# Summing the first pair's biases on ScalarE and queueing its query projection behind the spreading of 1/rms in a two-layer decoder trunk

## The chip, the cores and the metric

The kernel runs on one core of one Trainium2 chip. The metric is the device time of one launch in microseconds (us); three runs of the kernel before were timed, and one further execution was profiled. Engines are named as the profile names them: PE (TensorE matmul), PEld (its weight loads), DVE (VectorE), ACT (ScalarE), POOL (GpSimd) and SP (SyncE, which issues the DMAs here). "L178" is line 178 of the kernel before.

## The reference, cut to what matters

The input is a residual stream x of 1024 tokens by 1024 channels and a conditioning vector c. Layer A is a gated short convolution: modulated RMS norm, a projection to four parts, a causal convolution over three tokens, gates, an output projection, and the residual. Layer B is stick-breaking attention with 16 heads of 64 channels. Its keys and values come from a modulated norm of the same stream that layer B normalises.

```python
def modulated_norm(x, g, shift, scale):
    return rmsnorm(x, g) * (1.0 + scale[:, None, :]) + shift[:, None, :]
...
hkv = modulated_norm(x, kv_norm_g, kv_shift, kv_scale)
k_flat, v_flat = jnp.split(hkv @ w_kv, 2, axis=-1)
...
h = modulated_norm(x, norm_g, shift, scale)
q, z = jnp.split(h @ w_qz, 2, axis=-1)
...
return rmsnorm(x + gate[:, None, :] * (o @ w_out), final_norm_g)
```

## The kernel before, in words

Channels lie on the 128 partitions, tokens along the free dimension, in two halves of 512 tokens (`halves()`). Every matrix operand is split into a high and a low part in float32r, and a product is the sum of three matmuls (`linear`, L181 to L187): high weights by high activations (L185), high weights by low activations (L186), low weights by high activations (L187). One projection of 128 output channels over one half has 8 channel tiles, so 24 matmuls of 128x512, into one PSUM tile. PSUM tiles have four tags, "mm", "z", "tr" and "o", with two buffers each; `ps_any` goes round "mm", "z", "tr".

The change touches the seam between layer A's output projection and layer B's first pair of heads:

- The output projection of layer A (L432 to L457) runs per half over 8 output tiles. Each PSUM tile is added to the residual by DVE (L442), squared by ACT (L448), and the squares are summed by DVE (L450), all but those of the last tile.
- Then, in a high-priority block, `rms_columns` (L190) takes the column totals on PE: 8 matmuls of one column, four over the sum of the squares and four over the last tile's squares (L105; recorded as two groups). Twelve small DVE instructions follow (L202 to L209: a scaling, a shift, a subtraction, three Newton steps of three). `row_block` (L212) spreads the four columns of 1/rms over all partitions with four PE transposes (L215) and keeps the last of them as `last["pe"]`. DVE multiplies the eight residual tiles by it (L455), ACT rounds them to the high part x1h (L456), and DVE forms the low part x1l (L457).
- The weights of layer B's first pair (pair 0: keys, queries, values) are loaded while the second half of the output projection runs (`first_raw`, L460). `shift_terms` multiplies each by the modulation's shift and sums over the 8 channel tiles into a 128x128 tile (`bacc`), DVE multiplies the weights by the gain (L163), and `parts` (L469) splits them, ACT the high part and POOL the low part. The value weights' parts live in the attention pool, whose memory is that of layer A's tiles.
- A projection's bias is what is left of the shift: `shift_bias` (L174) transposes `bacc` on PE into a PSUM tile (L177), and DVE sums it along the free dimension (L178). `with_bias` (L494) hands it over as a function that is called at the first use. For pair 0 the PSUM tile has the tag "mm".
- `project_qkv(0)` (L567 to L573) walks the two halves: keys, queries, values. `evacuate` (L519) adds the bias, ACT for the high part (L521), DVE for the low part (L522); values go through ACT (L554), POOL (L556), four transposes (L559) and a second split. DMAs on SP's queue move the halves of the heads to their places (L517). In the first half the x1h and x1l that they read have long been made; in the second half they wait for L455 to L457.
- `attention` (L588) then takes the scores of a block of queries (L609, L610), the sigmoid on ACT (L614), a running product along the keys on DVE (L618), transposes (L628) and the product with the values (L642, L643).

The order of the instructions on each engine is laid out ahead of time by a planner: it takes the ready instruction of the highest priority (a high-priority block first, otherwise program order) by times that it models itself, and inserts the semaphores. Each engine then runs its list in order. `tc.issue_after(ins)` holds those instructions of its block that are on the engine of `ins` behind `ins` in that engine's list. `issue_after(last["x1"])` at L155 already keeps the next weights' DVE work behind L457.

Of the kernel before, what the change touches and what calls it, by code (L numbers as in the profile page):

```python
# [11 lines left out]
AF = mybir.ActivationFunctionType  # L12
ALU = mybir.AluOpType
AX = mybir.AxisListType.X

P = 128
# [21 lines left out]
def decoder_kernel(ctx, tc, vecs, xT, a_mod, kv_mod, b_mod, w_in, w_out_a, w_kv, w_qz, w_out_b, outT):  # L38
    nc = tc.nc
# [10 lines left out]
    last = {}  # L50

    def ps_tile(tag):
        return psum.tile([P, HALF], F32, name=f"ps_{tag}", tag=tag, bufs=PS_BUFS[tag])

    def ps_any():
        tags = ("mm", "z", "tr")
        seq[0] += 1
        return ps_tile(tags[seq[0] % len(tags)])
# [22 lines left out]
    def raw_tile():  # L81
        return wpool.tile([P, KT * P], F32, name="raw", tag="raw", bufs=3)
# [88 lines left out]
                acc, raw[:, kt * P:(kt + 1) * P], shift[:, kt:kt + 1], acc, op0=ALU.mult, op1=ALU.add)  # L171
        return acc

    def shift_bias(acc, tag):  # L174
        bias = const.tile([P, 1], F32, name="bias", tag="bias", bufs=8)
        ps = ps_tile(tag)
        nc.tensor.transpose(ps[:, :P], acc, ident)  # L177
        nc.vector.tensor_reduce(bias, ps[:, :P], AX, ALU.add)  # L178
        return bias

    def linear(ps, w, ah, al, sl, kts=range(KT)):  # L181
        hi, lo = w
        for kt in kts:
            wh, wl = hi[:, kt * P:(kt + 1) * P], lo[:, kt * P:(kt + 1) * P]
            nc.tensor.matmul(ps, lhsT=wh, rhs=ah[kt][:, sl], start=(kt == kts[0]), stop=False)  # L185
            nc.tensor.matmul(ps, lhsT=wh, rhs=al[kt][:, sl], start=False, stop=False)  # L186
            nc.tensor.matmul(ps, lhsT=wl, rhs=ah[kt][:, sl], start=False, stop=(kt == kts[-1]))  # L187


    def rms_columns(ssq, lo_t=0, hi_t=T, more=None, total=None):  # L190
# [36 lines left out]
    def halves():  # L227
        return [slice(h * HALF, (h + 1) * HALF) for h in range(NH)]
# [6 lines left out]
    def stile():  # L235
        return tmp.tile([P, HALF], F32, name="s", tag="s", bufs=11)
# [37 lines left out]
    for kt in range(KT):  # L274
# [16 lines left out]
        with tc.high_priority():  # L291
            for i in range(KT):
                nc.tensor.matmul(ssq[:, i:i + 1], lhsT=xr[:, i * P:(i + 1) * P], rhs=one,
                                 start=(kt == 0 and i == 0), stop=(kt == KT - 1 and i == KT - 1))
# [91 lines left out]
    for j in range(KT):  # L386
# [37 lines left out]
        if 2 <= j < 2 + len(PARTS):  # L424
            name, w, part, bcol, gcol = PARTS[j - 2]
# [6 lines left out]
    for sl in halves():  # L432
        ssq1 = tmp.tile([P, HALF], F32, name="ssq1", tag="graw", bufs=3)
        xs = []
        for j in range(KT):
            w = load_weights(w_out_a[j])[1:]
            xr = stile()
            xs.append(xr)
            nc.sync.dma_start(xr, xT[j * P:(j + 1) * P, sl])
            ps = ps_any()  # L440
            linear(ps, w, yh, yl, sl)
            nc.vector.scalar_tensor_tensor(xr, ps, mods["gate_a"][:, j:j + 1], xr, op0=ALU.mult, op1=ALU.add)  # L442
            nc.sync.dma_start(x1_dram[j, :, sl], xr)
            if j == 0:
                nc.scalar.activation(ssq1, xr, AF.Square)
            else:
                sq = tmp.tile([P, HALF], F32, name="sq1", tag="graw", bufs=3)
                nc.scalar.activation(sq, xr, AF.Square)  # L448
                if j < KT - 1:
                    nc.vector.tensor_add(ssq1, ssq1, sq)  # L450
        with tc.high_priority():

            scale = row_block(rms_columns(ssq1, 0, HALF, sq), 0, 4)
            for kt, x in enumerate(xs):
                nc.vector.tensor_mul(x, x, scale)  # L455
                nc.scalar.activation(x1h[kt][:, sl], x, AF.Copy)  # L456
                last["x1"] = nc.vector.tensor_tensor(x1l[kt][:, sl], x, x1h[kt][:, sl].bitcast(F32), op=ALU.subtract)  # L457
        if sl.start == 0:

            def first_raw(raw, w, m):  # L460
                nc.sync.dma_start(raw, w)
                return raw, scaled(raw, mods["gain_" + m], mods["shift_" + m])

            firsts = [
                first_raw(tmp.tile([P, D], F32, name="raw1", tag="gacc", bufs=1), w_kv[0], "kv"),
                first_raw(tmp.tile([P, 2 + T], F32, name="raw1", tag="v", bufs=2)[:, :T], w_qz[0], "b"),
                first_raw(raw_tile(), w_kv[NPAIR], "kv")]

    def parts(raw, pool=wpool, tags=("whi", "wlo"), bufs=2):  # L469
        hi, lo = (pool.tile([P, KT * P], F32R, name=n, tag=t, bufs=bufs) for n, t in zip(("whi", "wlo"), tags))  # L470
        split(hi, lo, raw, nc.gpsimd)
        return hi, lo

    first_w = [parts(raw) for raw, _ in firsts[:2]]
    papw.close()

# [17 lines left out]
    def with_bias(w, terms):  # L494
        bias = []

        def late():

            if not bias:
                bias.append(shift_bias(terms, "mm"))  # L500
            return bias[0]
        return w, late

    def projected(w, sl, ps_get=lambda: ps_tile("mm")):
        ps = ps_get()
        linear(ps, w, x1h, x1l, sl)
        return ps

    def half(a):
        return slice(a * DH, (a + 1) * DH)  # L510

    def project_qkv(p):
        def qk_tile(name):
            return att.tile([P, T], F32R, name=name, tag="qk", bufs=10)

        def move(dst, src):
            nc.sync.dma_start(dst.bitcast(F32), src.bitcast(F32))  # L517

        def evacuate(src, bias, hi, lo):  # L519
            bias = bias()  # L520
            nc.scalar.activation(hi, src, AF.Identity, bias=bias)  # L521
            nc.vector.scalar_tensor_tensor(lo, src, bias, hi.bitcast(F32), op0=ALU.add, op1=ALU.subtract)  # L522

        A, B = half(0), half(1)

        kl = [qk_tile("kl") for _ in range(2)]
        kh = [qk_tile("kh") for _ in range(2)]

        def keys(sl, t, bias):
            evacuate(t, bias, kh[0][:, sl], kl[0][:, sl])  # L530
            for k in (kh, kl):
                move(k[1][A, sl], k[0][B, sl])
                move(k[1][B, sl], k[0][B, sl])
                move(k[0][B, sl], k[0][A, sl])


        qq = [qk_tile("qq") for _ in range(2)]

        def queries(sl, t, bias):
            ql = att.tile([P, HALF], F32, name="ql", tag="pt", bufs=2).bitcast(F32R)  # L540
            evacuate(t, bias, qq[0][:, sl], ql)
            move(qq[1][B, sl], qq[0][B, sl])
            move(qq[1][A, sl], ql[B])
            move(qq[0][B, sl], ql[A])

        vv = []

        def values(sl, src, bias):

            if sl.start == 0:  # L550
                nc.gpsimd.memset(vt[:, :1], 0.0)
            else:
                nc.gpsimd.tensor_copy(vt[:, :1], vt[:, HALF:])
            nc.scalar.activation(vt[:, 1:], src, AF.Identity, bias=bias())  # L554
            t = att.tile([P, HALF], F32, name="dv", tag="pt", bufs=2)
            nc.gpsimd.tensor_tensor(t, vt[:, :HALF], vt[:, 1:], op=ALU.subtract)  # L556
            ps = ps_tile("tr")
            for i in range(4):
                nc.tensor.transpose(ps[:, i * P:(i + 1) * P], t[:, i * P:(i + 1) * P], ident)  # L559

            v = att.tile([P, 4, 4, DH], F32R, name="vv", tag="vv", bufs=4)
            src = ps.rearrange("p (b a d) -> p b a d", b=4, a=2)
            nc.scalar.activation(v[:, :, 0::3, :], src, AF.Copy)
            nc.vector.tensor_tensor(v[:, :, 1:3, :], src, v[:, :, 0::3, :].bitcast(F32), op=ALU.subtract)
            vv.append(v)

        if p == 0:  # L567
            first_w.append(parts(firsts[2][0], att, ("vv", "vv"), 4))
            (kw, kb), (qw, qb), (vw, vb) = (with_bias(w, terms) for w, (_, terms) in zip(first_w, firsts))
            for sl in halves():  # L570
                keys(sl, projected(kw, sl, ps_any), kb)
                queries(sl, projected(qw, sl, ps_any), qb)
                values(sl, projected(vw, sl, ps_any), vb)  # L573
        else:
            kw, kb = prepared(w_kv[p], mods["gain_kv"], mods["shift_kv"])
            for sl in halves():
                keys(sl, projected(kw, sl), kb)
            qw, qb = prepared(w_qz[p], mods["gain_b"], mods["shift_b"])
            for sl in halves():
                queries(sl, projected(qw, sl), qb)  # L580
            vw, vb = prepared(w_kv[NPAIR + p], mods["gain_kv"], mods["shift_kv"])
            for sl in halves():
                values(sl, projected(vw, sl), vb)
        return [(kh[a], kl[a], qq[a]) for a in range(2)], vv
# [152 lines left out]
    for j in range(EARLY):  # L737
        for sl in halves():
            ps = ps_any()
# [27 lines left out]
    for c, (a, b) in enumerate(CHUNKS):  # L767
        sl = slice(a, b)
# [51 lines left out]
```

## Time and profile before

| | us |
|---|---|
| three timed runs | 1450.73, 1195.78, 1192.18 |
| median of the three | 1195.78 |
| the profiled execution, its own time | 1193.45 |
| its span, first to last instruction | 1191.6 |

The time of the profiled execution and its span differ by 1.85 us, which lie outside the instructions. In that span PE is busy for 1160.2 us (97%), DVE for 857.4 (72%), ACT for 457.6 (38%) and POOL for 351.7 (30%); 36% of the time of the 16 DMA engines is used. The chain of work that ended last is PE for 86% and DVE for 10% of the span. Shares are averages over stages with different limits, so the seam has to be read from the timelines of the engines in its own stretch. A timeline row has start, length, engine, line, operation, output and inputs, shapes, count, and in brackets the idle time before it with what ended it. Matmuls overlap in it: each row's length holds the passage through the array, so the time that one takes on PE is the distance to the next start.

### The profile page before, as it was taken

What the parts mean: (1) busy time and instruction counts of PE and PEld (TensorE: products, weight loads), DVE (VectorE), ACT (ScalarE), POOL (GpSimd) and SP (SyncE); (2) the same over time, 40 slices, a digit from 0 to 9 for tenths busy, and PEclk for the clock granted to TensorE, in tenths of its full rate; (3) what the DMA queues carried; (4) which work ended last, traced back from release to release, by engine and by line L of the source; (5) the groups of instructions that cost most, each with busy time, mean ns of one, the idle gap of its engine ahead of it and who ended that gap; (6) DMA issues with size and microseconds to landing.
All of it is one profiled execution on the core that took longest, in us unless ns stands there. A gap on an engine that the chain in (4) does not pass through costs nothing.

```text
span 1191.6 us, 15883 instructions
## 1 busy us (share of the span) xinstructions
PE 1160.2 (97%) x6004; PEld 987.6 (83%) x6004; DVE 857.4 (72%) x1271; ACT 457.6 (38%) x750; POOL 351.7 (30%) x205
## 2 busy tenths in 40 slices
PE   7999999999999999989999999999999999999995
PEld 6888888888888888868888888888888888887885
DVE  7679325446546487478898898888988888686466
ACT  4344211212212224234544545444545444454341
POOL 3014423433433453321231322303123032121424
PEclk9799999999999999989999999999999999999997
DMA  9534315345354544342313223132241323562204
GB/s 373 220 123 144 104 54 165 109 151 176 99 167 150 193 141 154 114 100 70 86 65 89 63 78 99 64 85 67 63 107 53 84 67 79 143 248 88 71 1 141
DMA packets 61436, 138.47 MB, mean 116 GB/s; under 512 B 7472, under 2 KB 11696, under 8 KB 61360
## 3 DMA queue, kind: packets, MB, share of 16 engines
q1 hardware_dynamic: 61360, 137.46, 36.5%
q8 instruction: 47, 0.77, 0.3%
q14 instruction: 29, 0.24, 0.1%
HBM read 103.87 MB, written 14.68 MB: 99 GB/s over the span
## 4 chain that ended last, share of the span: by engine, by line
PE 86%; DVE 10%; issue 2%; ACT 1%; DMA 0%; DVEq 0%; SPq 0%; ACTq 0%
PE ps_mm L185 12%; PE ps_mm L186 12%; PE ps_mm L187 12%; PE ps_z L186 5%; PE ps_z L187 5%; PE ps_z L185 5%; PE ps_tr L186 5%; PE ps_tr L187 5%; PE ps_tr L185 5%; PE ps_tr L628 4%; DVE sfx L618 3%; PE ps_o L643 3%; PE ps_o L642 2%; PE ps_z L610 2%; PE ps_z L609 2%
## 5 line engine op out<-in xcount | busy, mean ns | idle before, releaser
L144 POOL TENSOR_TENSOR wlo<-raw,whi 128x1024 fp32r<-128x1024 f32 x87 | 219.4, 2523 | 632.9 <-ACT whi L143 516.2
L618 DVE TENSOR_TENSOR_SCAN sfx<-sfx,floor 128x128 f32<-128x128 f32 (+2 forms) x192 | 226.0, 1197 | 18.2 <-ACT sfx L614 18.2
L185 PE MATMUL ps_mm<-x1h,whi 128*128 128x512 f32 x480 | 191.7, 399 | 4.1 <-DVE bias L178 4.1
L186 PE MATMUL ps_mm<-x1l,whi 128*128 128x512 f32 x480 | 190.1, 396 | 0.0
L187 PE MATMUL ps_mm<-x1h,wlo 128*128 128x512 f32 x480 | 188.8, 393 | 0.0
L143 ACT ACTIVATE whi<-raw 128x1024 fp32r<-128x1024 f32 x87 | 92.1, 1059 | 144.1 <-issue 39.6
L631 ACT ACTIVATE ah<-ps_tr,minus 128x512 fp32r<-128x512 f32 (+1 forms) x160 | 100.4, 646 | 109.5 <-PE ps_tr L628 107.9
L632 DVE SCALAR_TENSOR_TENSOR al<-ps_tr,ah 128x512 fp32r<-128x512 f32 (+1 forms) x160 | 97.6, 623 | 41.7 <-ACT ah L631 41.2
L614 ACT ACTIVATE sfx<-ps_z 128x128 f32<-128x128 f32 (+2 forms) x192 | 90.4, 492 | 77.9 <-PE ps_z L610 76.2
L185 PEld LDWEIGHTS ps_mm<-x1h,whi 128*128 128x128 f32 x480 | 90.6, 189 | 22.2 <-DVE bias L178 5.1
L187 PEld LDWEIGHTS ps_mm<-x1h,wlo 128*128 128x128 f32 x480 | 90.6, 189 | 17.7
L121 DVE SCALAR_TENSOR_TENSOR gacc<-graw,cs,gacc 128x512 f32<-128x512 f32 x84 | 72.5, 885 | 44.9 <-DMA graw<-b_mod 22.1
L186 PEld LDWEIGHTS ps_mm<-x1l,whi 128*128 128x128 f32 x480 | 90.6, 189 | 16.6 <-DVE x1l L457 0.3
L628 PE MATMUL ps_tr<-ident,sfx 128*128 128x128 f32 x576 | 88.1, 274 | 0.0
L643 PE MATMUL ps_o<-al,vv 128*128 128x256 f32 x320 | 82.7, 294 | 4.3 <-DVE al L632 4.3
L642 PE MATMUL ps_o<-ah,vv 128*128 128x256 f32 x320 | 86.4, 282 | 0.1
L643 PEld LDWEIGHTS ps_o<-al,vv 128*128 128x128 f32 x320 | 60.4, 189 | 11.7 <-DVE al L632 8.7
L609 PE MATMUL ps_z<-kh,qq 128*128 128x128 f32 (+1 forms) x192 | 68.9, 364 | 0.7 <-ACT sfx L614 0.7
L642 PEld LDWEIGHTS ps_o<-ah,vv 128*128 128x128 f32 x320 | 60.5, 189 | 7.3 <-ACT ah L631 0.6
L628 PEld LDWEIGHTS ps_tr<-ident,sfx 128*128 128x128 f32 x576 | 65.5, 141 | 1.0
L610 PE MATMUL ps_z<-kl,qq 128*128 128x128 f32 (+1 forms) x192 | 65.3, 349 | 0.0
L185 PE MATMUL ps_mm<-nh,whi 128*128 128x512 f32 x152 | 59.4, 391 | 0.0
(277 smaller groups left out, 2435.0 us busy)
## 6 DMA issues: line engine op xcount, KB each, us to landing
raw<-w_in SPq DMA_DIRECT2D x29, 512.0 KB, 4.2
graw<-b_mod SPq DMA_DIRECT2D x48, 256.0 KB, 3.1
stage<-a_mod SPq DMA_DIRECT2D x16, 512.0 KB, 9.8
s<-xT SPq DMA_DIRECT2D x32, 256.0 KB, 4.8
graw<-kv_mod SPq DMA_DIRECT2D x32, 256.0 KB, 3.4
raw<-w_qz SPq DMA_DIRECT2D x16, 512.0 KB, 3.9
raw<-w_out_a SPq DMA_DIRECT2D x16, 512.0 KB, 3.5
raw<-w_kv SPq DMA_DIRECT2D x16, 512.0 KB, 3.6
```

Of the source, the lines that this page charges most:

```text
L143: nc.scalar.activation(hi, full, AF.Copy)
L144: lo_eng.tensor_tensor(lo, full, hi.bitcast(F32), op=ALU.subtract)
L185: nc.tensor.matmul(ps, lhsT=wh, rhs=ah[kt][:, sl], start=(kt == kts[0]), stop=False)
L186: nc.tensor.matmul(ps, lhsT=wh, rhs=al[kt][:, sl], start=False, stop=False)
L187: nc.tensor.matmul(ps, lhsT=wl, rhs=ah[kt][:, sl], start=False, stop=(kt == kts[-1]))
L609: nc.tensor.matmul(zps[:, :w], lhsT=qq[:, qs], rhs=kh[:, c0:c0 + w], start=True, stop=False)
L618: nc.vector.tensor_tensor_scan(rev, rev, floor[:, z0:z0 + w][:, ::-1], sf[r][:, s0 + w:s0 + w + 1], op0=ALU.mult, op1=ALU.max)
L628: nc.tensor.transpose(tp[:, s * P:(s + 1) * P], rows[r][:, jb * P - c0:(jb + 1) * P - c0], ident)
L631: nc.scalar.activation(ah[:, :w], tp[:, :w], AF.Identity, bias=minus)
L632: nc.vector.scalar_tensor_tensor(al[:, :w], tp[:, :w], -1.0, ah[:, :w].bitcast(F32), op0=ALU.add, op1=ALU.subtract)
L642: nc.tensor.matmul(ops[:, cols], lhsT=vs, rhs=ah[:, rs], start=first, stop=False)
L643: nc.tensor.matmul(ops[:, cols], lhsT=vs, rhs=al[:, rs], start=False, stop=end)
```

## The change

The bias of pair 0 is summed by an ACT copy with an accumulated output, in place of a DVE reduction; its PSUM tile has the tag "tr" in place of "mm". All three are traced right behind the second half's high-priority block, in a high-priority block of their own, with the transposes held behind the last matmul of the output projection. The two query projections of pair 0 (24 matmuls each) are held behind `last["pe"]`, the last transpose of the second half's spreading of 1/rms.

```diff
-    def shift_bias(acc, tag):
+    def shift_bias(acc, tag, eng=nc.vector):
         bias = const.tile([P, 1], F32, name="bias", tag="bias", bufs=8)
         ps = ps_tile(tag)
         nc.tensor.transpose(ps[:, :P], acc, ident)
-        nc.vector.tensor_reduce(bias, ps[:, :P], AX, ALU.add)
+        if eng is nc.scalar:
+            nc.scalar.activation(acc, ps[:, :P], AF.Copy, accum_out=bias)
+        else:
+            nc.vector.tensor_reduce(bias, ps[:, :P], AX, ALU.add)
         return bias
...
-            nc.tensor.matmul(ps, lhsT=wl, rhs=ah[kt][:, sl], start=False, stop=(kt == kts[-1]))
+            last["mm"] = nc.tensor.matmul(ps, lhsT=wl, rhs=ah[kt][:, sl], start=False, stop=(kt == kts[-1]))
...
+        out_last = last["mm"]
         with tc.high_priority():
...
+    with tc.high_priority(), tc.issue_after(out_last.ins):
+        first_b = [shift_bias(terms, "tr", nc.scalar) for _, terms in firsts]
     first_w = [parts(raw) for raw, _ in firsts[:2]]
...
-            (kw, kb), (qw, qb), (vw, vb) = (with_bias(w, terms) for w, (_, terms) in zip(first_w, firsts))
+            (kw, kb), (qw, qb), (vw, vb) = ((w, lambda b=b: b) for w, b in zip(first_w, first_b))
             for sl in halves():
                 keys(sl, projected(kw, sl, ps_any), kb)
-                queries(sl, projected(qw, sl, ps_any), qb)
+
+                with tc.issue_after(last["pe"].ins):
+                    q = projected(qw, sl, ps_any)
+                queries(sl, q, qb)
                 values(sl, projected(vw, sl, ps_any), vb)
```

## Rows read from the trace of the kernel before

**Rows 1.** Busy time of each engine over the whole span, from the page.

```profile
PE 1160.2 (97%) x6004; PEld 987.6 (83%) x6004; DVE 857.4 (72%) x1271; ACT 457.6 (38%) x750; POOL 351.7 (30%) x205
```

**Rows 2.** Stretches: PE, PEld, DVE, ACT, POOL busy; PE clock; DMA share; GB/s.

```profile
480.00:560.00 80.00, 75.62 (x350) 62.20 (x349) 51.41 (x99) 25.56 (x41) 21.23 (x13) 0.96 0.31 87
560.00:700.00 140.00, 138.91 (x789) 120.37 (x789) 126.39 (x191) 70.93 (x129) 38.11 (x24) 1.00 0.28 76
```

**Rows 3.** Timeline of PE across the seam.

```profile
494.14 0.39 PE L185 MATMUL ps_mm<-x1h,whi 128*128 128x512 f32 x1
...
494.60 0.27 PE L177 MATMUL ps_mm<-ident,bacc 128*128 128x128 f32 x1
494.71 0.95 PE L105 MATMUL ps_o<-one,ssq 128*128 128x1 f32 x8
...
500.18 0.94 PE L105 MATMUL ps_o<-one,sq 128*128 128x1 f32 x8
...
501.55 0.40 PE L185 MATMUL ps_z<-x1h,whi 128*128 128x512 f32 x1
...
507.14 0.60 PE L215 MATMUL ps_o<-ident,ry 128*128 128x128 f32 x4
507.69 0.33 PE L177 MATMUL ps_mm<-ident,bacc 128*128 128x128 f32 x1
509.18 0.50 PE L185 MATMUL ps_z<-x1h,whi 128*128 128x512 f32 x1 [1.17 <-ACT x1h L456]
512.90 0.80 PE L185 MATMUL ps_mm<-x1h,whi 128*128 128x512 f32 x1 [3.22 <-DVE bias L178]
...
517.93 0.63 PE L187 MATMUL ps_z<-x1h,wlo 128*128 128x512 f32 x1
```

**Rows 4.** Timeline of DVE across the seam.

```profile
501.17 0.16 DVE L202 TENSOR_SCALAR rv<-ps_o 128x4 f32<-128x4 f32 x1 [5.88 <-PE ps_o L105]
...
503.35 0.16 DVE L209 SCALAR_TENSOR_TENSOR ry<-rt,ry 128x4 f32<-128x4 f32 x1
507.34 0.29 DVE L178 TENSOR_REDUCE bias<-ps_mm 128x1 f32<-128x128 f32 x1 [3.83 <-PE ps_mm L177]
507.78 4.87 DVE L455 TENSOR_TENSOR s<-s,ps_o 128x512 f32<-128x512 f32 x8
...
512.77 7.12 DVE L457 TENSOR_TENSOR x1l<-s,x1h 128x512 fp32r<-128x512 f32 x8
```

**Rows 5.** Timeline of ACT, then of POOL, across the seam.

```profile
495.19 0.63 ACT L448 ACTIVATE sq<-s 128x512 f32<-128x512 f32 x1
508.50 4.81 ACT L456 ACTIVATE x1h<-s 128x512 fp32r<-128x512 f32 x8 [12.68 <-DVE s L455]
...
515.40 2.74 POOL L144 TENSOR_TENSOR wlo<-raw,whi 128x1024 fp32r<-128x1024 f32 x1 [17.65 <-DVE x1l L457]
```

**Rows 6.** The stalled stretch, PE alone: us, PE busy (x), PE clock, DMA share, GB/s.

```profile
507.69:518.36 10.67, 6.29 (x16) 0.68 0.12 25
```

**Rows 7.** Other stretches, columns as in rows 2, and a wait of PE near the end.

```profile
16.70:20.10 3.40, 2.37 (x10) 1.46 (x9) 2.95 (x2) 3.02 (x4) 2.29 (x1) 1.00 1.06 414
...
30.30:33.70 3.40, 3.40 (x12) 2.67 (x11) 0.04 (x1) 1.06 (x1) 0.00 (x0) 0.51 1.02 418
...
1177.20:1180.60 3.40, 1.97 (x12) 1.89 (x10) 2.44 (x5) 1.33 (x4) 2.45 (x3) 0.50 0.26 86
...
1176.58 0.40 PE L215 MATMUL ps_o<-ident,ry 128*128 128x128 f32 x2 [2.40 <-DVE ry L209]
```

**Rows 8.** Timelines of ACT, DVE and PE where pair 0's attention begins.

```profile
533.43 0.27 ACT L614 ACTIVATE sfx<-ps_z 128x128 f32<-128x128 f32 x1
...
535.28 0.29 DVE L168 TENSOR_SCALAR bacc<-raw,shift_b 128x128 f32<-128x128 f32 x1 [7.03 <-DMA raw<-w_qz]
...
538.24 0.48 DVE L618 TENSOR_TENSOR_SCAN sfx<-sfx,floor 128x128 f32<-128x128 f32 x1
...
549.90 0.49 PE L628 MATMUL ps_tr<-ident,sfx 128*128 128x128 f32 x3
```

## The prediction

> **What bounds the kernel now.** Start with the engines' shares on the page: PE is busy for 1160.2 of 1191.6 us [rows 1]. An average like that hides where the other 31 us lie, so the next view is the busy time by stretch: from 480 to 560 us PE is busy for 75.62 of 80, at a mean granted clock of 0.96, while in the 140 us that follow it is busy for 138.91 [rows 2]. So the seam between the layers is one of the few places where PE waits, and what follows is bound by PE: time that PE gains at the seam should reach the end.
>
> Then the timelines at the seam, PE first [rows 3]. PE starts pair 0's keys of the first half at 494.14, its queries at 501.55, the spreading of 1/rms (L215) at 507.14, a bias transpose at 507.69, and then it waits twice: 1.17 us for x1h and 3.22 us "for the bias" of L178. DVE's timeline says why both are late [rows 4]. The small chain that makes 1/rms runs from 501.17 to 503.51 (L202 to the last L209, 503.35 and 0.16), then DVE idles until 507.34: its result is ready, but the transposes that spread it stand in PE's list behind all 24 query matmuls. The multiplications L455 start at 507.78. The bias reductions stand in the same DVE list, the last of them behind those eight multiplications; until it has read its PSUM tile, the tag "mm" has no buffer for the keys of the second half. ACT, which makes x1h, idles for 12.68 us meanwhile [rows 5].
>
> The price of this: from the transpose at 507.69 to 518.36 is 10.67 us [rows 6]. In it lie that transpose (0.11, the distance from one such row to its neighbour at 494.60 and 494.71) and 13 projection matmuls, the first at 509.18, the last at 517.93 [rows 3]. A matmul takes (507.14 - 501.55 - 0.11) / 24 = 0.228 us at full clock. So the stretch holds 0.11 + 13 x 0.228 = 3.07 us of work and **7.6 us are lost**: about 4.9 to waiting up to 512.90, and 2.7 to the granted clock, which after the wait is at its lower level, 1.2 GHz (0.68 is the mean of the stretch).
>
> **The change part by part.**
>
> *Biases.* Removed from DVE: three reductions of 0.29 us [rows 4], 0.9 us in all. Added to ACT: three copies of 128x128 with an accumulated output. No such instruction is in this trace; the same shape without the accumulation takes 0.27 us, and the eight roundings of 128x512 take 4.81, or 0.60 each [rows 5, 8]. I bound one between 0.27 and 0.63 us (the squares' row), the three between 0.8 and 1.9, and take 1.2. They lie in ACT's idle stretch of 12.68 us, so they cost nothing; ahead of the last squares (0.63 us at 495.19) they could hold these back by 1.9 us, but the totals of these squares come on PE at 500.18, with over 4 us to spare. The three transposes stay, 0.11 us each on PE; two of them move from 507 to before the spreading, 0.22 us. They go through the tag "tr", whose buffer of the last output tile DVE empties at about 495; a wait on it could cost PE up to half a us, and is covered if the planner puts key matmuls between, as it did with the transpose at 494.60. I take 0.
>
> What comes free is the "mm" buffer of the second half's keys: they no longer wait for L178. What would be late next is x1l, one each 7.04 / 8 = 0.88 us from L457 [rows 4].
>
> *Queries behind the spreading.* Nothing is added, 24 + 24 matmuls are moved. After the keys of the first half PE has nothing that is ready: the value weights' low part waits for a buffer of layer A until 515.40 [rows 5], the second half waits for x1h. So PE now waits for the chain of small DVE instructions in the open. Step by step: the keys, both groups of totals and one transpose took until 501.55; two more transposes make 501.77. I take the totals of the last squares to come last in it (their ACT work now has the high-priority bias copies beside it, and PE passes only two more key matmuls after them anyway). From the end of the totals to the first small instruction is 501.17 - 500.18 - 0.81 = 0.18 us (0.81 as from 494.71 to the next matmul), the chain is 2.34, and a spreading follows its chain by some 0.14. So L215 starts at 501.77 + 0.18 + 2.34 + 0.14 = 504.43, not 507.14: **2.7 us earlier**, after a new wait of PE of 2.66 us. With the totals two matmuls from the end, as before, the wait is 2.2. If they came early enough to hide the chain behind the keys, it is 0; if DVE's low part of the first keys (0.6 to 0.9 us, as one of L455 or of L457) is put ahead of the chain, it is 3.4. These are the ends.
>
> Then DVE: L455 starts at 507.78 - 2.71 = 505.07, ends near 509.9, and the first x1l is there at 510.75. PE spreads (0.55), starts the queries at 504.98 and is done with them after 24 x 0.228 = 5.47, at 510.45. So the multiplications and roundings are now beside the queries, which is where the old waits of 4.9 us go. Keys and queries of the second half, taken in turn as before, need 6 x 0.228 = 1.37 us per channel tile against 0.88 from DVE: no further wait. The value weights come 2.7 us earlier too (512.7 + 2.74), with 10 us of keys and queries ahead of their use.
>
> *The clock.* After the wait of 2.40 us at 1176.58 the granted clock from 1177.20 is 0.50 [rows 7]. After the 1.03 us of waiting within 16.70 to 20.10 it stayed at 1.00. The new wait is 2.66 us with eight matmuls of a single column in front of it, so I expect the lower level. What it costs: a stretch such as 30.30 to 33.70, at 0.51, does half of its work, 1.7 us lost [rows 7]; the stall of before lost 2.7. I take 1.7, between 0 and 2.7.
>
> The Trainium skill speaks against this term, in "TensorE: Matmul & The Clock Gate", section "Why this matters for your kernels": it lets a pause of about this length between bursts pass without loss of clock. By that rule the term is 0 and the time is that of the second case below. This trace doesn't bear it out: the 2.40 us at 1176.58 were enough.
>
> *Sum.* Lost before 7.6. Lost after: 2.66 waiting + 1.7 clock = 4.36. Gain 7.6 - 4.36 = 3.25 us. The profiled execution took 1193.45 us, so 1193.45 - 3.25 = **1190.2 us**. The median of the three runs is 1195.78, 2.3 above it (one of the three is far off at 1450.73, and the lowest is 1192.18); I count from the profiled execution, whose rows these are, and let the range hold the difference.
>
> **Rivals.**
>
> *The clock doesn't fall.* For it: PE works at full rate right up to the totals, and a wait of 1.17 us alone did not lower the clock before 509.18. Against it: the 2.40 us. Gain 4.95, 1188.5 us.
>
> *The chain is hidden.* The planner puts the last totals early among the keys, since the squares are ready at 495.82; the spreading then interrupts the keys and PE never waits. Against it: before, they stood two matmuls from the end although nothing hindered them. Lost after some 0.3, gain 7.3: 1186.2 us.
>
> *The change hardly does what it says.* The bias copies are ready in ACT's list before the last squares, and the last transpose stands at the end of the keys; then squares, totals and chain all come behind it. Squares from 502.1 to 502.7, totals to 503.6, spreading at 506.2: a wait of 4.4 and the clock's 2.7 of before, together 7.1: 1192.9 us. Against it: the planner fills its list as buffers come free, so the transposes should be early.
>
> *Slower: pair 0's attention runs into DVE.* DVE's list there has bacc of L168 waiting 7.03 us for a weight transfer, until 535.28; the first running product L618 stands behind it, at 538.24, though its input from ACT was done at 533.70: 4.5 us late. PE doesn't notice, since the transposes that read it stand at 549.90, behind projections [rows 8]. The change re-deals PE's list from here on. If those transposes stand ahead of the remaining projections, PE waits up to 4.5 us: lost 4.36 + 4.5 = 8.9, 1.3 more than before: 1194.7 us. It decides from a wait of 3.25 us. Against it: the planner ranks by program order, and the weights' buffers and SP's moves come earlier as the rest does.
>
> **How the numbers follow.** Forecast 0.5, clock kept 0.2, chain hidden 0.08, hardly any effect 0.1, slower 0.12. The first two reach from 1188.5 to 1190.2, and the hidden chain and the slower case lie about 4 us to both sides; repeats of one kernel differ by 2 to 3 us (1192.18, 1193.45, 1195.78). The range is 1185.5 to 1195.5. Two per cent, about what a measurement of this kernel can tell from no change, are 24 us; every case lies within 8. Chances: faster by over that 0.02, within it 0.96, slower 0.02, the outer two for a re-dealt list that I can't see.
>
> **What would show it.** Right: L215 of the second half near 504.4 with a PE wait of 2 to 2.7 us before it, released by DVE ry; the L455 row 2.7 us earlier; no wait on L178 before the second half's keys; three ACT rows with bias before 500; DVE no longer idle between L209 and L455 for 3.8 us; a low-clock stretch of about 3.4 us from 504 to 508. Wrong: a wait before L215 far over 3 us, a new wait of PE on x1l behind the queries, or new waits of PE on L618 or L614 between 520 and 560. The prediction is wrong as a whole if the seam gains its 3 us and the busy time of PE from 560 on falls behind by as much.

## The result, and the profile after

Over 22 runs of each the median went from 1195.05 to **1188.5 us**; the ratio is 0.9948, 95% interval 0.9933 to 0.9962, so the kernel is 4 to 8 us faster here, which is within the two per cent. The forecast was 1190.2 in a range of 1185.5 to 1195.5. Line numbers after are higher than before: L181 is the old L178, L188 to L190 the old L185 to L187, L205 to L212 the old L202 to L209, L218 the old L215, L459 to L461 the old L455 to L457.

The profiled execution after took 1185.21 us, its span 1183.4. The page's first part and the busy time by stretch, columns as in [rows 1] and [rows 2], have PE at 98%, and in the stretch of the seam PE is busy for 2.9 us more than in [rows 2], at a clock of 1.00 where it was 0.96:

```profile
PE 1155.4 (98%) x6004; PEld 983.9 (83%) x6004; DVE 860.6 (73%) x1268; ACT 458.2 (39%) x756; POOL 352.6 (30%) x205
...
480.00:560.00 80.00, 78.51 (x381) 65.20 (x380) 58.37 (x108) 29.74 (x53) 20.30 (x12) 1.00 0.33 89
560.00:700.00 140.00, 139.32 (x798) 121.21 (x797) 129.58 (x188) 71.07 (x130) 40.44 (x24) 1.00 0.27 74
```

PE's timeline at the seam, to be read against [rows 3]:

```profile
492.11 0.27 PE L177 MATMUL ps_tr<-ident,bacc 128*128 128x128 f32 x1
492.14 0.48 PE L188 MATMUL ps_mm<-x1h,whi 128*128 128x512 f32 x1
...
497.95 0.95 PE L105 MATMUL ps_o<-one,sq 128*128 128x1 f32 x8
...
499.53 0.40 PE L190 MATMUL ps_mm<-x1h,wlo 128*128 128x512 f32 x1
501.42 0.62 PE L218 MATMUL ps_o<-ident,ry 128*128 128x128 f32 x4 [1.49 <-DVE ry L212]
501.80 0.48 PE L188 MATMUL ps_z<-x1h,whi 128*128 128x512 f32 x1
...
507.33 0.39 PE L188 MATMUL ps_mm<-x1h,whi 128*128 128x512 f32 x1
...
507.79 0.40 PE L189 MATMUL ps_mm<-x1l,whi 128*128 128x512 f32 x1
```

The queries (501.80) now follow the spreading, and the second half's keys (507.33) and their first product with x1l (507.79) start without a wait: both waits of [rows 3] are gone. One new wait stands in their place, 1.49 us before the spreading. Counted by starts, PE loses 501.42 - (499.53 + 0.23) = **1.66 us, against 7.6 before**. DVE's timeline, against [rows 4]:

```profile
498.93 0.16 DVE L205 TENSOR_SCALAR rv<-ps_o 128x4 f32<-128x4 f32 x1 [5.87 <-PE ps_o L105]
...
501.11 0.16 DVE L212 SCALAR_TENSOR_TENSOR ry<-rt,ry 128x4 f32<-128x4 f32 x1
502.08 4.87 DVE L459 TENSOR_TENSOR s<-s,ps_o 128x512 f32<-128x512 f32 x8 [0.81 <-PE ps_o L218]
506.87 7.13 DVE L461 TENSOR_TENSOR x1l<-s,x1h 128x512 fp32r<-128x512 f32 x8
```

The small chain takes the same 2.34 us, but the eight multiplications start 0.81 us behind its end; in [rows 4] they started 4.27 us behind it. ACT, against [rows 5]:

```profile
493.11 0.26 ACT L179 ACTIVATE bacc<-ps_tr 128x128 f32<-128x128 f32 x1
493.26 0.19 ACT L179 ACTIVATION_READ_ACCUMULATOR bacc<-ps_tr 128x1 f32 x1
493.36 0.62 ACT L451 ACTIVATE sq<-s 128x512 f32<-128x512 f32 x1
...
502.80 4.82 ACT L460 ACTIVATE x1h<-s 128x512 fp32r<-128x512 f32 x8 [4.76 <-DVE s L459]
```

A bias is a copy of 0.26 us and a reading of the accumulator of 0.19, overlapping. One of the three lies ahead of the last squares, two behind.

**What the span hides.** Between the two profiled executions the span shrank by 8.2 us, but 2.0 of it lie ahead of the seam: the first key matmul starts at 492.14 here and at 494.14 in [rows 3]. That is not the change. A second profile of the changed kernel has it at 497.34; the first 100 us of the two, columns as in [rows 2], then that matmul's row in the second:

```profile
0.00:100.00 100.00, 92.36 (x487) 79.62 (x488) 73.67 (x110) 42.54 (x54) 16.43 (x17) 0.91 0.61 226
```

```profile
0.00:100.00 100.00, 92.75 (x464) 80.79 (x465) 71.58 (x106) 41.73 (x52) 16.52 (x17) 0.86 0.57 216
...
497.34 0.48 PE L188 MATMUL ps_mm<-x1h,whi 128*128 128x512 f32 x1
```

The granted clock of the opening differs from execution to execution, 0.91 and 0.86, and by 100 us PE has issued 487 matmuls in the one and 464 in the other, so everything behind it is shifted. Over all thirteen profiles the first key matmul starts between 491.41 and 499.01 us, whatever the kernel. So below, "the rest" is the span less the start of that matmul, which leaves the opening out: before 1191.6 - 494.14 = 697.46 us, after 1183.4 - 492.14 = 691.26, **6.2 us less**. Over the further profiles of both kernels below, the difference lies between 3.9 and 6.2.

### The profile page after: what moved, and what is told of

Read it like the earlier page. It is cut to its first block, busy times and chain, and to the rows that moved or that the text cites. A ratio compares the mean times of both kernels' runs of the same rounds, so it can differ in the third digit from the quotient of the medians.

```text
span 1183.4 us, 15887 instructions
## 1 busy us (share of the span) xinstructions
PE 1155.4 (98%) x6004; PEld 983.9 (83%) x6004; DVE 860.6 (73%) x1268; ACT 458.2 (39%) x756; POOL 352.6 (30%) x205
## 4 chain that ended last, share of the span: by engine, by line
PE 86%; DVE 11%; issue 2%; ACT 1%; DMA 0%; DVEq 0%; SPq 0%
PE ps_mm L188 12%; PE ps_mm L190 12%; PE ps_mm L189 12%; PE ps_z L190 5%; PE ps_z L189 5%; PE ps_z L188 5%; PE ps_tr L189 5%; PE ps_tr L190 5%; PE ps_tr L188 5%; PE ps_tr L637 4%; DVE sfx L627 3%; PE ps_o L652 3%; PE ps_o L651 2%; PE ps_z L619 2%; PE ps_z L618 2%
## 5 line engine op out<-in xcount | busy, mean ns | idle before, releaser
L144 POOL TENSOR_TENSOR wlo<-raw,whi 128x1024 fp32r<-128x1024 f32 x87 | 220.8, 2540 | 607.1 <-ACT whi L143 504.7
L188 PE MATMUL ps_mm<-x1h,whi 128*128 128x512 f32 x480 | 190.9, 398 | 0.4 <-DVE bias L181 0.4
L190 PE MATMUL ps_mm<-x1h,wlo 128*128 128x512 f32 x480 | 188.2, 392 | 0.0
L641 DVE SCALAR_TENSOR_TENSOR al<-ps_tr,ah 128x512 fp32r<-128x512 f32 (+1 forms) x160 | 97.1, 623 | 38.7 <-ACT ah L640 38.3
L623 ACT ACTIVATE sfx<-ps_z 128x128 f32<-128x128 f32 (+2 forms) x192 | 90.4, 491 | 82.9 <-PE ps_z L619 81.9
L188 PEld LDWEIGHTS ps_mm<-x1h,whi 128*128 128x128 f32 x480 | 90.2, 188 | 18.3 <-DVE bias L181 1.1
L190 PEld LDWEIGHTS ps_mm<-x1h,wlo 128*128 128x128 f32 x480 | 90.3, 188 | 17.4
L188 PE MATMUL ps_mm<-nh,whi 128*128 128x512 f32 x152 | 59.4, 391 | 0.0
```

What stands on the lines that cost most here:

```text
L144: lo_eng.tensor_tensor(lo, full, hi.bitcast(F32), op=ALU.subtract)
L190: last["mm"] = nc.tensor.matmul(ps, lhsT=wl, rhs=ah[kt][:, sl], start=False, stop=(kt == kts[-1]))
L641: nc.vector.scalar_tensor_tensor(al[:, :w], tp[:, :w], -1.0, ah[:, :w].bitcast(F32), op0=ALU.add, op1=ALU.subtract)
```

## The experiments

The rest, the spreading's distance from the first key matmul, and the timing of each kernel. The timings come from four sessions, the later three on three chips, each against its own runs of the kernel before; the second and third profile of the longer chain and the second of the kernel before weren't timed further.

| kernel | rest, us | spreading after, us | ratio to the kernel before (95%) |
|---|---|---|---|
| before; again | 697.46; 696.60 | 13.00; 13.02 | |
| changed; again; a third time | 691.26; 692.74; 691.36 | 9.28; 9.28; 9.27 | 0.9948 (0.9933 to 0.9962); 0.9926 (0.9902 to 0.9951); 0.9981 (0.9959 to 1.0003) |
| queries not held | 697.44 | 13.10 | 0.9979 (0.9961 to 0.9996) |
| biases late, on DVE | 694.51 | 9.93 | 0.9972 (0.9951 to 0.9994) |
| biases early, on DVE | 691.30 | 9.29 | 0.9936 (0.9913 to 0.9958) |
| longer chain, three profiles | 694.28; 695.69; 696.59 | 10.46 each | 0.9997 (0.9981 to 1.0012) |
| split keys, two profiles | 690.70; 690.59 | 6.27; 6.27 | 0.9928 (0.9901 to 0.9954); 0.9949 (0.9926 to 0.9973) |

**The kernel before, again.**

> The kernel before, once more, for a second profile. Theory: the seam repeats (waits of 1.2 and 3.2 us, then a lower clock; 13 us from the first key matmul to the spreading) within 0.1 us, and what differs between two profiles of one kernel is the time of the first key matmul itself, by the low-clock stretches of the first 100 us. Rival (the seam itself varies by some us): the waits or the low stretch differ by more than 1 us.

PE's waits at the seam:

```profile
513.66 0.50 PE L185 MATMUL ps_z<-x1h,whi 128*128 128x512 f32 x1 [1.17 <-ACT x1h L456]
517.38 0.80 PE L185 MATMUL ps_mm<-x1h,whi 128*128 128x512 f32 x1 [3.22 <-DVE bias L178]
```

They repeat to 0.01 us. The rest differs by 0.9, because the low clock lasted longer in the first profile, 6.8 us against 3.4. By the prediction's own count, the seam lost 6.7 us in this profile (512.16 to 521.92, of which 3.07 are work), not 7.6. So an effect on the rest under 1 us needs a look at the rows, and the times of single runs tell little.

**The changed kernel, again and a third time.**

> The changed kernel once more, for the clock at the seam. Theory: of the 6 us that the median moved, about 5.9 us come from the seam (7.6 us lost before, 1.7 us lost after) as long as the clock stays at its upper level there, and about 4 us when a wait of 1.5 us with single-column matmuls ahead of it lowers the clock. So the wait before the spreading is 1.3 to 1.8 us again, released by DVE ry, and a low clock may or may not follow it; the ratio is 0.9933 to 0.9965. Rival (the profiled execution was only lucky in its start): the seam takes the same time as in the kernel before, and the ratio is 0.998 to 1.001.

> The changed kernel a third time, timed on the same chip as the next one, and a third look at the clock behind the wait of 1.49 us. Theory: the wait repeats within 0.1 us and the clock is 1.00 behind it, as in the two profiles of it and in the one with the sums on DVE. Rival (whether the clock falls depends on the moment at which the wait comes, not on its length alone): this profile shows a stretch at the lower level behind it, and the time from the first key matmul to the end is 1.5 to 2 us longer.

The wait before the spreading is 1.49 and 1.48 us and the clock is 1.00 behind it, both times. The rest of the second profile is 1.4 us longer; it has two waits of PE on L641 (the old L632, in the attention), of 0.84 and 0.88 us, that the other two have not. The ratios of the three sessions run from 0.9926 to 0.9981, and the interval of the third reaches 1.0003, so that session alone doesn't separate the kernel from the one before. The variation of the opening is as large as the effect. The median is lower in each session, by 6.6, 8.6 and 2.8 us, and the 40 runs together have one of 1189.75.

**Queries not held.**

```diff
-                with tc.issue_after(last["pe"].ins):
-                    q = projected(qw, sl, ps_any)
+                q = projected(qw, sl, ps_any)
```

> The changed kernel without holding the queries behind the spreading; early biases on ACT stay. Theory (the order of the spreading is what pays): PE spreads after the queries again, some 3.5 us later, and although the keys of the second half need not wait for a bias, they wait for x1h and x1l: 5 to 5.5 us of waiting in two pieces, the second released by DVE x1l, and a lower clock after it; ratio 0.998 to 1.001. Rival (the gain came from the PSUM buffer that the bias reductions held): most of the gain stays, one wait of 1 to 2 us, ratio 0.994 to 0.997.

PE's waits, and the multiplications on DVE:

```profile
510.76 0.60 PE L218 MATMUL ps_o<-ident,ry 128*128 128x128 f32 x4
512.80 0.50 PE L188 MATMUL ps_mm<-x1h,whi 128*128 128x512 f32 x1 [1.44 <-ACT x1h L460]
516.92 0.80 PE L189 MATMUL ps_mm<-x1l,whi 128*128 128x512 f32 x1 [3.39 <-DVE x1l L461]
...
511.39 4.87 DVE L459 TENSOR_TENSOR s<-s,ps_o 128x512 f32<-128x512 f32 x8 [4.59 <-PE ps_o L218]
```

The biases come early and no key waits for one, yet PE waits 4.83 us, now for x1l, and the rest is that of the kernel before. The wait that the trace of before put down to the bias was covering the one on x1l: freeing the PSUM buffer alone shows no gain in the profile. The timing doesn't say the same: its ratio lies at the edge of the theory's range, and its interval, 0.9961 to 0.9996, has a gain of 0.5 to 4.7 us. On the same chip the changed kernel's median is 6.8 us lower (1187.66 against 1194.44), so most of the gain needs the hold; whether the early biases alone give a small one stays open.

**Biases late.** The early sums are taken out, and `with_bias` is used for pair 0 as before; the queries stay held.

```diff
-    with tc.high_priority(), tc.issue_after(out_last.ins):
-        first_b = [shift_bias(terms, "tr", nc.scalar) for _, terms in firsts]
...
-            (kw, kb), (qw, qb), (vw, vb) = ((w, lambda b=b: b) for w, b in zip(first_w, first_b))
+            (kw, kb), (qw, qb), (vw, vb) = (with_bias(w, terms) for w, (_, terms) in zip(first_w, firsts))
```

> The changed kernel with the biases of pair 0 as before (DVE, tag mm, at first use); the queries stay behind the spreading. Theory: the spreading comes some 3 us earlier as in the changed kernel, and the last bias reduction, behind the eight multiplications on DVE, is done about when PE ends the queries; the keys wait under 1 us for it. Ratio 0.9935 to 0.997, within 1 us of the changed kernel. Rival (the PSUM buffer pays): the wait of 3 us on the bias is still there and the ratio is 0.998 to 1.001.

PE at the spreading, DVE's reductions, and the stretch behind it (columns as in [rows 2]):

```profile
499.61 0.27 PE L177 MATMUL ps_mm<-ident,bacc 128*128 128x128 f32 x1
500.26 0.33 PE L177 MATMUL ps_mm<-ident,bacc 128*128 128x128 f32 x1 [0.39 <-DVE bias L181]
502.12 0.62 PE L218 MATMUL ps_o<-ident,ry 128*128 128x128 f32 x4 [1.53 <-DVE ry L212]
...
499.92 0.29 DVE L181 TENSOR_REDUCE bias<-ps_mm 128x1 f32<-128x128 f32 x1
500.63 0.29 DVE L181 TENSOR_REDUCE bias<-ps_mm 128x1 f32<-128x128 f32 x1
...
502.96:506.37 3.41, 3.41 (x10) 2.62 (x9) 3.41 (x6) 2.87 (x5) 0.00 (x0) 0.50 0.01 2
```

No wait on the bias is left before the second half's keys, as the theory had it, and half of the gain in the rest is there (2.1 to 3.0 us). The other half is lost in a way that I had not expected: two reductions stand inside the small chain on DVE (499.23 to 501.97, 2.74 us where it was 2.34), PE waits in two pieces, the spreading comes 0.65 us later, and behind it the clock is at 0.50 for 3.41 us, 1.7 us lost. A wait of 0.64 us on the old L632, at 629.53, which the changed kernel doesn't have, makes up most of what is left. "Within 1 us of the changed kernel" was wrong: the rest is 3.2 us longer, and 1.7 of these come from a fall of the clock that need not follow each time, as the longer chain below shows.

**Biases early, on DVE.**

```diff
-        first_b = [shift_bias(terms, "tr", nc.scalar) for _, terms in firsts]
+        first_b = [shift_bias(terms, "tr") for _, terms in firsts]
```

> The changed kernel with the three early biases summed by DVE in place of ACT, everything else the same. Theory: DVE is idle there too, so three reductions of 0.29 us before 499 us cost nothing; the wait before the spreading stays at 1.3 to 1.8 us and the ratio is that of the changed kernel, 0.9933 to 0.9965. Rival (taking the sums off DVE is part of the gain): the small chain of 1/rms starts later by up to 0.9 us, the wait before the spreading grows by as much, the ratio is 0.001 higher.

DVE's reductions and chain, then PE's wait:

```profile
493.44 0.28 DVE L181 TENSOR_REDUCE bias<-ps_tr 128x1 f32<-128x128 f32 x1
497.81 0.49 DVE L181 TENSOR_REDUCE bias<-ps_tr 128x1 f32<-128x128 f32 x2 [4.09 <-PE ps_tr L177]
499.41 0.16 DVE L205 TENSOR_SCALAR rv<-ps_o 128x4 f32<-128x4 f32 x1 [1.11 <-PE ps_o L105]
...
501.89 0.62 PE L218 MATMUL ps_o<-ident,ry 128*128 128x128 f32 x4 [1.47 <-DVE ry L212]
```

The sums are done 1.1 us before the chain needs DVE, and wait and rest are those of the changed kernel. What counts of the biases is when they are summed, not the engine. The three experiments together, by the rest: the hold without the early biases gains 2.1 to 3.0 us, the early biases without the hold nothing, both together 3.9 to 6.2.

**Longer chain.** Two more Newton steps in the second half's 1/rms of layer B, to give the wait the length that the prediction had.

```diff
-    def rms_columns(ssq, lo_t=0, hi_t=T, more=None, total=None):
+    def rms_columns(ssq, lo_t=0, hi_t=T, more=None, total=None, steps=3):
...
-        for _ in range(3):
+        for _ in range(steps):
...
-            scale = row_block(rms_columns(ssq1, 0, HALF, sq), 0, 4)
+            scale = row_block(rms_columns(ssq1, 0, HALF, sq, steps=5 if sl.start else 3), 0, 4)
```

> The changed kernel with five Newton steps in place of three in the second half's 1/rms of layer B: six more small DVE instructions in front of the spreading, 1.2 us by the distance of 0.2 us between them. It sets the wait to the length that the prediction gave it. Theory (a wait of 1.5 us does not lower the clock, one of some 2.7 us does): wait before the spreading 2.6 to 2.8 us, then a stretch at the lower level of 3 to 7 us; from the start of the first key matmul to the end of the program 2.5 to 4.5 us longer than in the changed kernel. Rival (the clock stays up after 2.7 us too, so the prediction's clock term had no ground): only the 1.2 us are added, the clock is 1.00 from there on.

> The longer chain, a second profile, for the clock behind a wait of 2.66 us. Theory (the moment decides): the clock falls in some of the profiles of this kernel and not in others; the first showed none, its twelve timed runs lie 6 us above the changed kernel's where its profile lost 3. Rival (it never falls after so short a wait in mid-kernel): 1.00 again in this and the next.

> The longer chain, a third profile, the same question as in the second: a stretch of 3.4 us at the lower level behind the wait in at least one of the two if the moment decides, in neither if the length does.

The wait and the stretch behind it in the three profiles of this one kernel, columns as in [rows 2]:

```profile
507.48 0.62 PE L218 MATMUL ps_o<-ident,ry 128*128 128x128 f32 x4 [2.66 <-DVE ry L212]
...
507.50:514.30 6.80, 6.80 (x32) 5.70 (x33) 6.16 (x11) 5.44 (x9) 0.00 (x0) 1.00 0.00 1
```

```profile
504.47 0.90 PE L218 MATMUL ps_o<-ident,ry 128*128 128x128 f32 x4 [2.66 <-DVE ry L212]
...
504.70:508.10 3.40, 3.40 (x11) 2.78 (x10) 2.69 (x5) 1.97 (x4) 0.00 (x0) 0.50 0.01 2
508.10:511.50 3.40, 3.40 (x16) 2.79 (x15) 3.40 (x7) 3.40 (x6) 0.00 (x0) 1.00 0.00 0
```

```profile
509.47 1.08 PE L218 MATMUL ps_o<-ident,ry 128*128 128x128 f32 x4 [2.66 <-DVE ry L212]
...
507.90:514.70 6.80, 5.23 (x15) 4.30 (x16) 5.29 (x15) 3.39 (x6) 0.00 (x0) 0.50 0.00 1
```

With the same wait, 2.66 us, the clock stayed up once, went to the lower level for 3.4 us once, and for 6.8 us once, with a rest of 694.28, 695.69 and 696.59. So the fall costs 1.4 and 2.3 us here by the rest; by the rows it is half of the time that PE is busy at the lower level, 1.7 of 3.40 and 2.6 of 5.23. The length of the wait doesn't decide it alone. In the second profile the fall comes just behind the wait, at 504.7. In the third it comes at 507.9, 1.1 us after the wait began and 1.6 before it ended, so a wait of 1.49 us that began at the same moment would have had the fall in it too. By the timing (0.9997) the longer chain gives the whole gain back. The first profile's rest is still 3.0 us over the changed kernel's: 1.2 are the chain, the other 1.8 lie behind the seam, where the planner laid out another list and PE waits 0.20 us on L623 (the old L614) at 542.76 and 0.64 us on L641 at 634.12; what makes up the remaining 1 us stays open.

**Split keys.** The idea that follows from the wait: bring the last totals ahead of most of the first half's keys, and keep two channel tiles of these for after the spreading. `last["tot"]` is the last matmul of `column_totals`, and `linear` takes two flags for where the sum begins and ends.

```diff
...
-                keys(sl, projected(kw, sl, ps_any), kb)
+                if sl.start == 0:
+                    k = ps_any()
+                    linear(k, kw, x1h, x1l, sl, range(2), closes=False)
+                    with tc.issue_after(last["tot"].ins):
+                        linear(k, kw, x1h, x1l, sl, range(2, 6), opens=False, closes=False)
+                    with tc.issue_after(last["pe"].ins):
+                        linear(k, kw, x1h, x1l, sl, range(6, KT), opens=False)
+                else:
+                    k = projected(kw, sl, ps_any)
+                keys(sl, k, kb)
```

> The changed kernel with pair 0's first-half keys cut in three: two channel tiles ahead of the last column totals, four behind these, two behind the spreading. Theory (the chain of 1/rms is now the only open wait at the seam): the totals come 3 us earlier, the small chain lies beside 12 key matmuls, the wait before the spreading falls from 1.49 to under 0.4 us, and the time from the first key matmul to the end of the program is 1 to 1.7 us shorter than in the changed kernel; ratio to the kernel before about 0.0012 lower than that of the changed kernel. Rival (the next thing late takes its place): the wait before the spreading goes, but PE waits as long for x1l behind the queries, or at the bias transposes ahead of the totals, and the time stays within 0.5 us.

> The split keys again, against the changed kernel on the same chip. Theory: no wait before the spreading, 687.0 to 687.5 us from the first key matmul to the last instruction of an engine, the median 0.5 to 2.5 us under that of the changed kernel. Rival (the wait at the start of pair 1's attention gives it all back): medians within 0.5 us.

PE at the seam, DVE's multiplications, and a wait of PE later, in the second profile:

```profile
494.00 0.95 PE L105 MATMUL ps_o<-one,sq 128*128 128x1 f32 x8
...
497.45 0.39 PE L190 MATMUL ps_mm<-x1h,wlo 128*128 128x512 f32 x1
497.68 0.60 PE L218 MATMUL ps_o<-ident,ry 128*128 128x128 f32 x4
498.04 0.48 PE L188 MATMUL ps_mm<-x1h,whi 128*128 128x512 f32 x1
...
498.32 4.87 DVE L459 TENSOR_TENSOR s<-s,ps_o 128x512 f32<-128x512 f32 x8 [0.98 <-PE ps_o L218]
...
624.84 0.38 PE L661 MATMUL ps_o<-al,vv 128*128 128x256 f32 x1 [0.64 <-DVE al L650]
```

PE no longer waits at the seam, the spreading comes 3 us earlier, and 1.66 us are saved there. Of these 0.64 go to a wait in the attention that the changed kernel doesn't have. The rest ends 0.6 to 0.8 us under the first and third profiles of the changed kernel (2.0 to 2.2 under the second), less than the 1 to 1.7 expected. Counted to the last instruction of an engine, as the second expectation has it, the two rests are 687.09 and 686.99 us. On the same chip as the third session the medians are 1189.71 against 1190.46, which two intervals that overlap don't separate. By the rows it is the best of the versions here; by the timing that isn't shown.

## Why the prediction was right

The direction and the mechanism held, and the time lies in the range. Point by point:

- *Biases cost nothing on ACT.* Right. Two instructions each, 0.34 to 0.38 us from the start of the one to the end of the other, in ACT's idle time. The one ahead of the last squares holds these back by some 0.2 us, and their totals come 4 us later. Summing on DVE gave the same.
- *The new wait of PE, 2.66 us.* Right in kind, off in size: 1.66 us lost. Chain (2.34) and spreading behind it (0.15 against 0.14) are as worked out; the step that failed is "I take the totals of the last squares to come last". They start 5.81 us after the first key matmul, not later than the 6.04 of before, with four key matmuls behind them where two were, so 1.0 us (498.76 to 499.76) of the 2.66 from the totals to the spreading is covered. The spreading comes 3.7 us earlier than before, not 2.7.
- *The clock falls, 1.7 us.* Wrong for this kernel: 1.00 behind the wait in all three profiles of it and in the one with the sums on DVE, four of four. The row the term rested on, a wait of 2.40 us with a fall behind it [rows 7], is no rule for the seam: with 2.66 us the fall came in two profiles of three, and its cost, 1.4 and 2.3 us, was well bounded by "between 0 and 2.7". At its own place, near the end, the wait (2.38 to 2.40 us) has a fall beside it in all thirteen profiles, but from 0.2 us before its end to 2.9 us after, and a further wait of PE follows there. Four of four at 1.49 us doesn't show that so short a wait is safe, since the third profile of the longer chain fell 1.1 us into its wait. The Trainium skill's rule ("TensorE: Matmul & The Clock Gate", "Why this matters for your kernels") gave the right answer here, no loss after 1.49 us; the longer chain, with a fall in two profiles of three at 2.66 us, shows that it isn't safe up to the pause that it allows.
- *No further wait on x1l behind the queries.* Right, the row at 507.79.
- *Sum.* 4.36 us were forecast as lost and 1.66 measured, so the seam gives 5.9 and not 3.25, or 5.0 if the 6.7 us of the second profile of before are taken. The rest gained 6.2. Behind the seam one more wait is gone, the 0.48 us that PE spent on L178 at 637.95, for pair 2's keys. The likeliest case was thus not the one that came; the second, with the clock kept, is the nearest. That it had 1188.5, the measured median, is luck, and so is part of the nearness of 1190.2: both were counted from 1193.45, and the median of the kernel before turned out at 1195.05. The gain of the medians is 6.55 us, twice the 3.25 that were forecast.
- *Rivals.* The hidden chain is what the split keys bring about by hand. "The change hardly does what it says" didn't come: the last bias transpose is at 497.37, and the last totals stand at 497.95, ahead of the end of the keys. The slower case, pair 0's attention running into DVE, didn't come: the first running product [rows 8] now starts before the weights' wait, which is 3.40 us and not 7.03, and PE has no wait there:

```profile
525.42 1.84 DVE L627 TENSOR_TENSOR_SCAN sfx<-sfx,floor 128x128 f32<-128x128 f32 x1
...
530.66 0.29 DVE L168 TENSOR_SCALAR bacc<-raw,shift_b 128x128 f32<-128x128 f32 x1 [3.40 <-DMA raw<-w_qz]
```

## What to carry to other kernels

An instruction that a whole chain hangs on (here four transposes) goes ahead of bulk work that could run later, even if the bulk engine must idle for it: 1.66 us of open wait bought back 6.7 to 7.6. When a trace blames one releaser, ask what would be late next: without the hold, the early bias only turned a wait for the bias into one for x1l. And compare from a mark behind the opening when the opening's clock varies by more than the effect.

## What was not expected of the hardware

- The opening's granted clock varies from execution to execution (0.86 to 0.91 over the first 100 us in two profiles of one kernel) and moves the seam: its first key matmul starts at 491.41 us at the earliest and 499.01 at the latest over thirteen profiles.
- One and the same wait of PE (2.66 us) leaves the clock at 2.4 GHz in one execution and has it at 1.2 GHz for 3.4 or 6.8 us in others, in one of them from 1.1 us after the wait began. A wait of 0.39 and one of 1.53 us, one transpose apart, were followed by 3.41 us at 1.2 GHz in another kernel. What decides between them isn't settled by these runs.
- A sum on ACT shows as two instructions, the copy (0.26 to 0.28 us at 128x128) and ACTIVATION_READ_ACCUMULATOR (0.19 to 0.20 us).
